# Soft mixture of experts: the first rows of x loaded in float32 on two hardware queues and cast on chip, with the opening matmuls in another order

## The chip, the cores and the metric

The kernel runs on one core of a Trainium2 chip. The metric is the device time of one execution in microseconds (us): the median of three runs. The profile is of one further execution, taken by the hardware profiler. Engines: TensorE (PE; PEld is its weight load), VectorE (DVE), ScalarE (ACT), GpSimd (POOL) and SyncE (SP). DMAs are issued by SyncE and ScalarE (hardware queues) and by GpSimd (a software queue, the only one used here for DMAs that change the type).

## What is computed

```python
# x: 16 x 512 x 512, router_logits: 16 x 512 x 8, expert_weights: 8 x 512 x 2048, all float32
probs = softmax(router_logits)             # over the 8 experts
for e in range(n_experts):
    expert_out = np.matmul(x, expert_weights[e])
    output += probs[:, :, e:e+1] * expert_out
```

Every row of x is scaled by each of its eight probabilities, and the eight scaled copies side by side (8 x 512 = 4096 columns) are multiplied by the stacked weights (4096 x 2048).

## The kernel before

All products are of float16 operands with float32 sums in PSUM. The 8192 rows are cut into 32 blocks of HQ = 256, and the whole multiplication is done by a fast scheme of seven block products at two levels (Strassen-Winograd). So x, weights, and sums and differences of weights are needed in many combinations; VectorE forms these while TensorE multiplies. That main part begins at about 42 us, has its order written out (from line 334 on), and is not changed in its text.

The change is in the opening, which is planned by hand:

- A zero tile is set on VectorE, and ten products of it (WARM, lines 84 to 89) run on TensorE into PSUM that is used by nothing else.
- Two small constants follow: ident (lines 209 to 212, set on VectorE, made an identity by GpSimd) and ones (line 257).
- The logits of the first four groups of 128 rows (lg0[0]) come in one DMA on SyncE (line 206). Rows 0 to 255 and 512 to 767 of x come in two DMAs of GpSimd (lines 207 and 208), which cast float32 to float16 on their way into the tile xs0. j numbers the groups: j = 0 and 1 are the first 256 rows, j = 2 and 3 the others.
- GpSimd then issues the first weights: the block b11[0, 0] for expert 0 in two halves (chunks c = 0, 1 and c = 2, 3 of 128 input columns), then whole experts. Two more casts of x (j = 4 to 7, lines 217 and 218) and further weights follow on the same queue.
- early_p(0) makes the softmax of these rows: VectorE with one exp on ScalarE.
- diag(p) writes, for one expert, four diagonal matrices of probabilities (ident times p), 128 x 512 in all.
- early_z0(e, d) makes, for expert e and each j, four small products (128 x 128) of x with such a diagonal. Their result in one bank of PSUM is x transposed and scaled. It is copied to z0[j] in float16, by VectorE for even j, by ScalarE for odd j (evacuate).
- Then comes the loop over n = 0, 1 (two column blocks of NB = 512) and e = 0 to 3 (HE = 4 experts). For each e, 16 large products (128 x 512), c outside and j inside, add z0[j] times the weights into four banks ps[j]. Before the change the small products of experts 0 and 1 stand ahead of the loop, those of experts 2 and 3 ahead of the large products of experts 0 and 1 of n = 0.
- At e = 2 of n = 0 the code writes down the two other softmaxes on VectorE: early_p(1), for j = 4 to 7, and softmax_of_all, for the logits of all rows. Their logits are loaded by load_logits on SyncE. softmax_of_all ends in two casts on ScalarE (lines 296 and 297) and four stores of the probabilities (p_dram) on SyncE.
- At the end of each n ScalarE copies the four banks out (line 331), and SyncE stores them (kept).
- In n = 1, behind the large products of experts 0 and 1, early_xp1 transposes x for j = 4 to 7 with ident, and spreads their probabilities with a product with ones (two banks for each j).

VectorE's and ScalarE's instructions of these helpers keep the order in which the code writes them (keep_in_program_order); TensorE executes in order too. PSUM has eight banks of 128 x 512 float32. bank() takes the next free one, and an instruction that needs a bank waits for whoever still reads it.

Of the kernel before, what the change touches and what calls it, by code (L numbers as in the profile page):

```python
# [31 lines left out]
def kernel(  # L32
# [7 lines left out]
    nc = tc.nc  # L40
    P = 128
    f16 = mybir.dt.float16
    f32 = mybir.dt.float32
# [3 lines left out]
    B, S, H = x.shape  # L47
    E, _, EH = expert_weights.shape
    T = B * S
    C = H // P  # L50
    HE = E // 2
    NB = 512
    NH = EH // 2
    WARM = 10
    HQ = 256
# [4 lines left out]
    x_f = x.flatten_outer_dims()  # L60
# [3 lines left out]
    wpool = ctx.enter_context(tc.tile_pool(name="wpool", bufs=15))  # L64
# [4 lines left out]
    cpool = ctx.enter_context(tc.tile_pool(name="cpool", bufs=1))  # L69
# [4 lines left out]
    def h_tile(shape, dtype):  # L74
        return hpool.tile(shape, dtype, name="h", tag="h")

    def half():
        return h_tile([P, NB], f32)

    tiny = cpool.tile([P, 1], f32, name="tiny")  # L80
    nc.vector.memset(tiny, 0.0)
    nc.scalar.activation(out=tiny, in_=tiny, func=mybir.ActivationFunctionType.Exp)

    with tc.tile_pool(name="psum0", bufs=1, space=bass.MemoryType.PSUM) as psum0:
        zero = h_tile([P, NB], f16)
        nc.vector.memset(zero, 0.0)
        every = psum0.tile([P, 8, NB], f32, name="every")
        for i in range(WARM):
            nc.tensor.matmul(every[:, i % 8, :], zero[:, 0:P], zero, start=True, stop=True)
# [5 lines left out]
    def note(i):  # L95
        last[i.ins.engine] = i.ins
        if ordered[0]:
            tc.keep_in_program_order(i)

    def dve(i):  # L100
        last[i.ins.engine] = i.ins
        tc.keep_in_program_order(i)

    act = dve
# [12 lines left out]
    def sp(o, i):  # L117
        note(nc.sync.dma_start(out=o, in_=i))

    def pool(o, i, **how):  # L120
        note(nc.gpsimd.dma_start(out=o, in_=i, **how))  # L121

    def bank():
        return psum.tile([P, NB], f32, name="ps", tag="ps")

    def mm(ps, z, w, start, stop):
        note(nc.tensor.matmul(ps, z, w, start=start, stop=stop, skip_group_check=True))  # L127
# [3 lines left out]
    def new_w():  # L131
        return wpool.tile([P, K8, NB], f16, name="w", tag="w")
# [31 lines left out]
    def inner_sums(b, t7=None):  # L164

        w = {1: b[0, 0], 2: b[1, 0], 3: b[1, 1], 7: t7 or b[0, 1]}

        def step(p, x, y):
            if p not in w:
                w[p] = new_w()  # L170
            tt(w[p], x, y, SUB)
        return w, {5: lambda: step(5, b[0, 1], b[0, 0]), 6: lambda: step(6, b[1, 1], w[5]),
                   4: lambda: step(4, b[1, 0], w[6]), 7: lambda: step(7, b[1, 1], b[0, 1])}
# [13 lines left out]
    lg_f = router_logits.flatten_outer_dims()  # L187
    P1, P2, PQ = 0, HE, 2 * HE

    xs0 = new_w()  # L190

    ROWS = ("(p j) h -> p j h", "(j p) h -> p j h")

    def cast_x(j):
        pool(xs0[:, ds(j, 2), :], x_f[ds(j * HQ, HQ), :].rearrange(ROWS[j // 4], p=P))

    def load_lg0(t):
        rows = lg_f.rearrange("(q h) e -> q h e", h=2 * HQ)[ds(2 * t, 2), 0:HQ]
        tile_ = lg0[t].rearrange("p (q j) e -> p q j e", j=2)
        if t == 0:  # L200
            sp(tile_, rows.rearrange("q (p j) e -> p q j e", p=P))
        else:
            for q in range(2):
                sp(tile_[:, q], rows[q].rearrange("(j p) e -> p j e", p=P))
    lg0 = [cpool.tile([P, 4, E], f32, name=f"lg0_{t}") for t in range(2)]
    load_lg0(0)
    cast_x(0)
    cast_x(2)
    ident = cpool.tile([P, P], f16, name="ident")
    nc.vector.memset(ident, 1.0)  # L210
    nc.gpsimd.affine_select(out=ident, in_=ident, compare_op=mybir.AluOpType.is_equal, fill=0.0, base=0,
                            pattern=[[-1, P]], channel_multiplier=1)
    b11 = {kn: new_w() for kn in BLOCKS}
    with behind():
        for kn in BLOCKS[:3]:
            cast_block(11, kn, b11[kn], 2 if kn == (0, 0) else 1)
    cast_x(4)
    cast_x(6)
    cast_block(11, BLOCKS[3], b11[BLOCKS[3]])

    def early_p(t):
        if t == 0:
            return softmax(lg0[t], 4, cpool.tile([P, HE, 4], f16, name="ph0"))
        pf = softmax(lg0[t], 4, cpool.tile([P, HE, 4], f32, name="pf0"))
        odd = pf.rearrange("p e (q j) -> p e q j", j=2)[:, :, :, 1]
        tt(odd[:, 0:2], odd[:, 0:2], odd[:, 2:4], ADD)
        ph = cpool.tile([P, HE, 4], f16, name="ph1")
        dve(nc.vector.tensor_copy(ph, pf))
        return ph

    def diag(p):

        d = h_tile([P, 4, P], f16)
        tt(d, ident.unsqueeze(1).to_broadcast([P, 4, P]), p.to_broadcast([P, 4, P]), MUL)
        return d

    def evacuate(o, ps, i):
        if i % 2:
            act(nc.scalar.copy(o, ps))
        else:  # L240
            dve(nc.vector.tensor_copy(o, ps))  # L241

    z0 = [zpool.tile([P, HE, C, P], f16, name="z", tag="z") for j in range(4)]
    ph0 = [early_p(0)]

    def diag_e(e):
        return diag(ph0[0][:, e].unsqueeze(2))

    def early_z0(e, d):
        for j in range(4):  # L250
            ps = bank()
            for c in range(C):
                mm(ps[:, ds(c * P, P)], xs0[:, j, ds(c * P, P)], d[:, j], c == 0, c == C - 1)
            evacuate(z0[j][:, e], ps.rearrange("p (c t) -> p c t", c=C), j)
# [5 lines left out]
    def diag_j(j):  # L260
        return diag(ph0[1][:, :, ds(j % 4, 1)])

    def early_xp1(j, d):
        t, rows = j // 2 - 2, ds(j % 2 * P, P)
        ps = bank()
        for c in range(C):
            mm(ps[:, ds(c * P, P)], xs0[:, j, ds(c * P, P)], ident, c == 0, c == C - 1)
        evacuate(xp1[t][0][:, :, rows], ps.rearrange("p (c t) -> p c t", c=C), 0)
        ps = bank()
        mm(ps, ones, d.rearrange("p e t -> p (e t)"), True, True)  # L270
        evacuate(xp1[t][1][:, :, rows], ps.rearrange("p (e t) -> p e t", e=HE), 1)
# [7 lines left out]
    def load_logits():  # L279
        dve(nc.vector.memset(lg_all[:, 0, 0:1], 0.0))  # L280
        dve(nc.vector.memset(lg0[1][:, 0, 0:1], 0.0))  # L281
        load_lg0(1)
        for r in range(R):
            sp(lg_all[ds(r * NHQ, NHQ)], lg_v[r])

    def softmax_of_all():

        pf = softmax(lg_all, J, h_tile([P, E, J], f32))
        pq = h_tile([P, HE, J], f32)
        tt(pq, pf[:, 0:HE], pf[:, HE:E], ADD)  # L290
        low = ds(P // 2, P // 2)
        pv = pf.rearrange("p (s e) j -> p s e j", s=2)[low]
        tt(pv[:, :, 0:2], pv[:, :, 0:2], pv[:, :, 2:4], ADD)
        tt(pq[low, 0:2], pq[low, 0:2], pq[low, 2:4], ADD)
        ph = h_tile([P, 3 * HE, J], f16)
        act(nc.scalar.copy(ph[:, 0:E], pf))
        act(nc.scalar.copy(ph[:, E:], pq))
        for r in range(R):
            sp(p_dram[:, :, ds(r * J, J)], ph[ds(r * NHQ, NHQ)])

    kept = [dram.tile([2, HQ, NB], f32, name=f"kept_{i}") for i in range(NI)]

    ds_ = [diag_e(0), diag_e(1)]
    early_z0(0, ds_[0])
    ds_.append(diag_e(2))
    load_logits()
    early_z0(1, ds_[1])
    for n in range(2):
        ps = [bank() for _ in range(4)]
        for e in range(HE):  # L310
            if n == 0 and e < 2:
                early_z0(e + 2, ds_[e + 2])
                if e == 0:
                    ds_.append(diag_e(3))
            if n == 0 and e == 2:
                ph0.append(early_p(1))
                ds_ = [diag_j(j) for j in range(4, 8)]
                softmax_of_all()
                w, sums = inner_sums(b11, new_w())
            for c in range(C):  # L320
                for j in range(4):
                    mm(ps[j], z0[j][:, e, c], b11[e // 2, n][:, e % 2 * C + c, :],
                       e + c == 0, e == HE - 1 and c == C - 1)
            if n == 1:
                for j in ((4, 5), (6, 7), (), ())[e]:
                    early_xp1(j, ds_[j - 4])
                if e == 1:
                    sums[5]()
        for j in range(4):
            o = half()  # L330
            act(nc.scalar.copy(o, ps[j]))
            sp(kept[j // 2][n].rearrange("(p j) m -> j p m", j=2)[j % 2], o)
# [706 lines left out]
```

## Time and profile before

| | |
|---|---|
| Median of three runs | 1377.12 us (1376.21 to 1377.82) |
| Profiled execution | 1377.86 us |
| Its span, from first to last instruction | 1376.2 us |
| TensorE busy | 1368.5 us (99%), 6390 matmuls |
| VectorE, ScalarE, GpSimd busy | 1108.8, 183.3, 412.3 us |
| Granted TensorE clock | 1.000 of full speed |

The opening in stretches: length, then TensorE's and VectorE's busy time and number of instructions, and the mean busy share of the 16 DMA engines (slightly over 1 where packets overlap).

| Stretch, us from the start | length | TensorE | VectorE | DMA share |
|---|---|---|---|---|
| 0.00 to 2.00 | 2.00 | 0.71 (2) | 0.61 (4) | 0.02 |
| 2.00 to 4.00 | 2.00 | 2.00 (6) | 0.86 (5) | 0.70 |
| 4.00 to 5.60 | 1.60 | 1.60 (5) | 1.35 (3) | 1.04 |
| 5.60 to 6.80 | 1.20 | 0.93 (9) | 0.40 (1) | 0.99 |
| 6.80 to 8.50 | 1.70 | 1.51 (24) | 1.45 (3) | 1.03 |
| 8.50 to 9.70 | 1.20 | 1.01 (16) | 1.20 (5) | 1.22 |
| 9.70 to 12.40 | 2.70 | 2.70 (15) | 1.95 (4) | 1.23 |
| 12.40 to 14.00 | 1.60 | 1.60 (19) | 0.35 (1) | 1.33 |

How to read it: matmuls are pipelined and the ends that the profile gives them are modelled, so a busy TensorE isn't TensorE at its peak. What counts is how far apart the starts of matmuls are. A line of the timeline has a start, a duration, the engine, the line of the code, the operation, and what it writes and reads; "x16" merges sixteen equal instructions, and the bracket tells how long the engine was idle before and what ended that. The chain of work goes back from the last instruction, at each step to what released it; a long chain through one engine means that this engine sets the end.

### The profile page before, as it was taken

How to read it: one execution, taken by the hardware profiler on the slowest of the kernel's cores; microseconds unless marked ns; L12 is line 12 of the kernel's file. 1: busy time of each engine (PE TensorE's matmuls, PEld its weight loads, DVE VectorE, ACT ScalarE, POOL GpSimd, SP SyncE). 2: the span in 40 equal slices, each digit the busy share in tenths (PEclk: the TensorE clock that was granted, in tenths of full speed). 3: DMA queues.
4: the chain of work that ended last, by engine and by line, in shares of the span. 5: the costliest groups of instructions: out<-in, count | busy, mean ns of one | idle time of the engine just before them, and what ended most of it. 6: DMA issues, size and time to landing. Idle time of an engine off the chain costs nothing.

```text
span 1376.2 us, 17481 instructions
## 1 busy us (share of the span) xinstructions
PE 1368.5 (99%) x6390; PEld 622.3 (45%) x6390; DVE 1108.8 (81%) x1290; ACT 183.3 (13%) x317; POOL 412.3 (30%) x652
## 2 busy tenths in 40 slices
PE   9999999999999999999999999999999999999998
PEld 4444444444444444444444444444444444444444
DVE  5846757679789888798887988889888898898782
ACT  3222111100011111111111100000000000222221
POOL 3222333231223342334332122333323322232321
PEclk9999999999999999999999999999999999999999
DMA  9997999999898998999897997988888979998785
GB/s 186 229 255 207 212 250 260 252 297 381 235 311 267 279 282 249 267 260 264 252 275 255 348 383 208 241 233 207 232 231 231 231 219 309 228 197 186 167 147 101
DMA packets 191271, 338.02 MB, mean 246 GB/s; under 512 B 52944, under 2 KB 86992, under 8 KB 187472
## 3 DMA queue, kind: packets, MB, share of 16 engines
q0 software_dynamic: 88688, 185.12, 55.8%
q1 hardware_dynamic: 98464, 123.34, 31.1%
q10 hardware_dynamic: 4032, 28.44, 5.3%
q8 instruction: 50, 0.82, 0.2%
q14 instruction: 37, 0.30, 0.1%
HBM read 207.65 MB, written 156.43 MB: 265 GB/s over the span
## 4 chain that ended last, share of the span: by engine, by line
PE 91%; issue 4%; DMA 3%; POOL 1%; DVE 1%; POOLq 0%; ACT 0%; DVEq 0%
PE ps L127 91%; POOL out_dram L121 1%; DMA out_dram<-h 1%; DMA w<-wd 1%; DMA w<-in_x_dram 0%; DVE h L107 0%; DVE z L107 0%; DVE u L107 0%; POOL wd L121 0%; DVE z L241 0%; POOL w L121 0%; ACT h L991 0%; POOLq L121 0%; DVEq L107 0%; DVE lg L281 0%
## 5 line engine op out<-in xcount | busy, mean ns | idle before, releaser
L127 PE MATMUL ps<-w,z 128*128 128x512 f16 x5416 | 1177.5, 379 | 2.1 <-DVE h L107 1.7
L127 PEld LDWEIGHTS <-z 128*128 128x128 f16 x5416 | 529.7, 98 | 639.8 <-issue 2.6
L121 POOL DMA_DIRECT2D out_dram<-h x380 | 249.2, 675 | 742.5 <-ACT h L536 369.1
L107 DVE TENSOR_TENSOR h<-ps,h 128x512 f32<-128x512 f32 x415 | 282.6, 688 | 207.8 <-PE ps L127 190.1
L107 DVE TENSOR_TENSOR z<-xT,pT 128x2048 f16<-128x2048 f16 x220 | 267.2, 1218 | 12.1 <-DMA xT<-xs 8.3
L127 PE MATMUL ps<-w,d 128*128 128x512 f16 x880 | 199.1, 379 | 0.0
L127 PEld LDWEIGHTS <-d 128*128 128x128 f16 x880 | 86.1, 98 | 103.8
L107 DVE TENSOR_TENSOR z<-z,d 128x2048 f16<-128x2048 f16 x110 | 132.2, 1217 | 0.0
L107 DVE TENSOR_TENSOR w<-w 128x1024 f16<-128x1024 f16 (+2 forms) x92 | 101.0, 1103 | 6.3 <-DMA wd<-w 3.9
L525 ACT COPY h<-ps 128x512 f32<-128x512 f32 x90 | 52.9, 587 | 375.0 <-PE ps L127 314.0
L536 ACT COPY h<-ps 128x512 f32<-128x512 f32 x64 | 37.6, 587 | 486.1 <-PE ps L127 459.7
L107 DVE TENSOR_TENSOR d<-z 128x1024 f16<-128x1024 f16 x110 | 75.4, 686 | 6.8 <-PE ps L127 5.0
L107 DVE TENSOR_TENSOR z<-z,u 128x2048 f16<-128x2048 f16 x64 | 78.4, 1225 | 2.2
L107 DVE TENSOR_TENSOR u<-xT,pT 128x2048 f16<-128x2048 f16 x64 | 78.0, 1219 | 0.0
L522 ACT COPY h<-ps 128x512 f32<-128x512 f32 x90 | 52.8, 587 | 173.8 <-PE ps L127 160.2
L121 POOL DMA_DIRECT2D wd<-w x86 | 48.4, 586 | 36.9 <-DVE w L107 27.4
L121 POOL DMA_DIRECT2D w<-in_expert_weights_dram x65 | 48.9, 783 | 34.2 <-DMA wd<-w 24.1
L107 DVE TENSOR_TENSOR ps<-ps,h 128x512 f32<-128x512 f32 (+1 forms) x66 | 45.4, 689 | 12.9 <-PE ps L127 12.9
L121 POOL DMA_DIRECT2D kept<-h x56 | 30.9, 551 | 75.5 <-ACT h L525 46.9
L107 DVE TENSOR_TENSOR h<-h 128x512 f32<-128x512 f32 (+2 forms) x69 | 45.1, 675 | 0.2
L518 ACT COPY ps<-ps 128x512 f32<-128x512 f32 x45 | 25.7, 572 | 114.6 <-PE ps L127 114.6
L107 DVE TENSOR_TENSOR z<-z 128x2048 f16<-128x2048 f16 x32 | 39.2, 1225 | 1.1
(47 smaller groups left out, 98.1 us busy)
## 6 DMA issues: line engine op xcount, KB each, us to landing
out_dram<-h POOLq DMA_DIRECT2D x380, 256.0 KB, 6.2
pT<-p_dram SPq DMA_DIRECT2D x140, 256.0 KB, 6.1
w<-wd ACTq DMA_DIRECT2D x27, 1024.0 KB, 9.8
h<-kept SPq DMA_DIRECT2D x100, 256.0 KB, 5.8
xT<-x SPq DMA_DIRECT2D x87, 256.0 KB, 5.8
wd<-w POOLq DMA_DIRECT2D x72, 256.0 KB, 5.8
w<-in_expert_weights_dram POOLq DMA_DIRECT2D x35, 512.0 KB, 10.1
h<-out_dram SPq DMA_DIRECT2D x68, 256.0 KB, 5.5
```

Source lines behind the costliest of these rows:

```text
L107: dve(nc.vector.tensor_tensor(out=o, in0=a, in1=b, op=op))
L121: note(nc.gpsimd.dma_start(out=o, in_=i, **how))
L127: note(nc.tensor.matmul(ps, z, w, start=start, stop=stop, skip_group_check=True))
L518: act(nc.scalar.copy(self.banks["b"], x))
L522: act(nc.scalar.copy(o[tn], q if p == 5 else x))
L525: act(nc.scalar.copy(o[TN[p]], b if p == 2 else x))
L536: act(nc.scalar.copy(o[tn], b))
```

## The change

- The two logits halves (128 x 16 each) and the two halves of x (256 rows each, 512 KB) for j = 0 to 3 are issued ahead of everything else, one of each on ScalarE's queue (j = 0, 1) and on SyncE's queue (j = 2, 3). x lands in float32 in the tile x32.
- GpSimd's two casting DMAs for these rows go; four copies cast x32 into xs0 instead, on ScalarE for j = 0 and 2, on VectorE for j = 1 and 3.
- The zero tile is kept (in the pool of the weights). In the built program its set stands on VectorE behind those of ident and ones.
- The small products of expert 0 are split in two groups: j = 0, 1, then three products of the zero tile; j = 2, 3, then one more.
- The 16 large products of expert 0 of n = 0 go by quarters (c = 0, 1 with j = 0, 1; c = 0, 1 with j = 2, 3; then the same with c = 2, 3). The small products of expert 1 stand after the first eight, those of expert 2 after the sixteen, those of expert 3 after the large ones of expert 1.

```diff
+    lg0 = [cpool.tile([P, 4, E], f32, name=f"lg0_{t}") for t in range(2)]
+    x32 = wpool.tile([P, 4, H], f32, name="x32", tag="w")
+    for q, begin in enumerate((nc.scalar, nc.sync)):
+        rows = ds(2 * q * HQ, HQ)
+        begin.dma_start(out=lg0[0][:, ds(2 * q, 2), :],
+                        in_=router_logits.flatten_outer_dims()[rows].rearrange("(p j) e -> p j e", p=P))
+        begin.dma_start(out=x32[:, ds(2 * q, 2), :], in_=x_f[rows, :].rearrange("(p j) h -> p j h", p=P))
     tiny = cpool.tile([P, 1], f32, name="tiny")
...
-        zero = h_tile([P, NB], f16)
+        zero = wpool.tile([P, NB], f16, name="zero", tag="w")
...
     def cast_x(j):
-        pool(xs0[:, ds(j, 2), :], x_f[ds(j * HQ, HQ), :].rearrange(ROWS[j // 4], p=P))
...
-    load_lg0(0)
-    cast_x(0)
-    cast_x(2)
+        pool(xs0[:, ds(j, 2), :], x_f[ds(j * HQ, HQ), :].rearrange("(j p) h -> p j h", p=P))
+
     ident = cpool.tile([P, P], f16, name="ident")
...
-    def early_z0(e, d):
-        for j in range(4):
+    def early_z0(e, d, js=range(4)):
+        for j in js:
...
-        load_lg0(1)
+        for q in range(2):
+            sp(lg0[1][:, ds(2 * q, 2), :], lg_f[ds((4 + 2 * q) * HQ, HQ)].rearrange("(j p) e -> p j e", p=P))
...
-    ds_ = [diag_e(0), diag_e(1)]
-    early_z0(0, ds_[0])
-    ds_.append(diag_e(2))
+    QUARTERS = [(c, j) for g in range(2) for h in range(2)
+                for c in (2 * g, 2 * g + 1) for j in (2 * h, 2 * h + 1)]
+    ORDERS = [(c, j) for c in range(C) for j in range(4)], QUARTERS
+
+    def cast_x32(j):
+        if j % 2:
+            dve(nc.vector.tensor_copy(xs0[:, j, :], x32[:, j, :]))
+        else:
+            act(nc.scalar.copy(xs0[:, j, :], x32[:, j, :]))
+
+    ds_ = [diag_e(0)]
+    for h in range(2):
+        for j in (2 * h, 2 * h + 1):
+            cast_x32(j)
+        early_z0(0, ds_[0], (2 * h, 2 * h + 1))
+        for i in range(3 - 2 * h):
+            mm(bank(), zero[:, 0:P], zero, True, True)
     load_logits()
-    early_z0(1, ds_[1])
+    ds_ += [diag_e(1), diag_e(2)]
     for n in range(2):
         ps = [bank() for _ in range(4)]
         for e in range(HE):
-            if n == 0 and e < 2:
-                early_z0(e + 2, ds_[e + 2])
-                if e == 0:
-                    ds_.append(diag_e(3))
+            if n == 0 and e == 1:
+                ds_.append(diag_e(3))
...
-            for c in range(C):
-                for j in range(4):
-                    mm(ps[j], z0[j][:, e, c], b11[e // 2, n][:, e % 2 * C + c, :],
-                       e + c == 0, e == HE - 1 and c == C - 1)
+            for c, j in ORDERS[n == 0 and e == 0]:
+                mm(ps[j], z0[j][:, e, c], b11[e // 2, n][:, e % 2 * C + c, :],
+                   e + c == 0, e == HE - 1 and c == C - 1)
+                ahead = {(0, 1, 3): 1, (0, 3, 3): 2, (1, 3, 3): 3}.get((e, c, j))
+                if n == 0 and ahead:
+                    early_z0(ahead, ds_[ahead])
```

## The prediction

> **What bounds the kernel now.** I read the page's chain of work first, then the chain in order of time, then the timeline of the first 29 us, then the landing times of DMAs.
>
> ```profile
> PE 91%; issue 4%; DMA 3%; POOL 1%; DVE 1%; POOLq 0%; ACT 0%; DVEq 0%
> ```
>
> TensorE sets the end. So time changes only where its stream of matmuls waits. In order of time:
>
> ```profile
> 2.00 4.86 DMA w<-in_x_dram
> ...
> 7.35 0.69 DVE z L241
> 8.04 0.60 DVE h L107
> ...
> 8.69 51.37 PE ps L127 x272
> ```
>
> Up to 8.7 us x and VectorE lead; after that TensorE alone. The timeline (start, duration) of the opening:
>
> ```profile
> 0.97 0.27 DVE L86 MEMSET h<- 128x256 uint32 x1
> 1.21 0.17 DVE L210 MEMSET ident<- 128x128 f16 x1
> 1.29 4.45 PE L89 MATMUL every<-h 128*128 128x512 f16 x10 [1.29 <-DVE h L86]
> ...
> 2.90 5.24 POOL L121 DMA_DIRECT2D w<-in_expert_weights_dram  x7
> ...
> 5.64 0.77 PEld L127 LDWEIGHTS <-w 128*128 128x128 f16 x8 [0.80 <-DMA w<-in_x_dram]
> ...
> 6.91 1.51 PE L127 MATMUL ps<-h,w 128*128 128x128 f16 x24 [0.33 <-DMA w<-in_x_dram]
> ...
> 7.57 1.56 ACT L239 CAST z<-ps 128x512 f16<-128x512 f32 x3 [0.36 <-PE ps L127]
> ...
> 9.75 2.27 PEld L127 LDWEIGHTS <-z 128*128 128x128 f16 x12 [0.17 <-DMA w<-in_expert_weights_dram]
> ```
>
> Spacing, from count and duration less the last one's (0.22 small, 0.38 large, 0.63 warming, single rows): a warming product 0.424, a small one (1.51-0.22)/23 = 0.056, a large one 0.216 (51 in 11.17). 48 small products end the opening; the first large one starts at 9.76, held 0.15 by its weights, and no wait follows in this stretch. Then the part that no chain shows, because it is just in time:
>
> ```profile
> 13.64 1.29 DVE L241 CAST z<-ps 128x512 f16<-128x512 f32 x2 [2.00 <-PE ps L127]
> ...
> 15.19 0.19 DVE L177 TENSOR_REDUCE h<-lg 128x4 f32<-128x32 f32 x1 [0.26 <-DMA lg<-in_router_logits_dram]
> ...
> 24.82 0.62 ACT L296 CAST h<-h 128x512 f16<-128x512 f32 x1 [3.37 <-DVE h L107]
> ...
> 25.65 2.04 ACT L331 COPY h<-ps 128x512 f32<-128x512 f32 x4
> ...
> 27.93 0.39 PE L127 MATMUL ps<-ident,w 128*128 128x128 f16 x4
> ```
>
> VectorE runs both remaining softmaxes without a break from 15.19; ScalarE's casts (L296) wait for their end; behind these, in order, stand the four copies (L331) that empty the banks of n = 0; early_xp1 takes these banks at 27.93. The first copy ends at 25.65+0.58 = 26.23: 1.7 us of slack.
>
> **The change, part by part. The start.** The zero tile is now set behind the two other constants on VectorE. Their spacing is 0.14 (L210 at 1.21, the next at 1.35), so it is 0.28 late: warming starts at 1.58, and its ten products hold TensorE until 1.58+10x0.427 = 5.85 (without the last one's tail).
>
> **x.** Two issues, the logits' first, stand on ScalarE and SyncE. Logits took 0.46 and the next SyncE issue stood at 1.33, so both halves of x are issued near 1.33. On ScalarE some 0.9 us of issuing goes ahead of the table load (1.28): exp moves from 3.18 to about 3.35, hidden, since its diagonal is ready near 5.0 and TensorE is busy to 5.85. Neither two such loads nor a 4 KB piece of float32 stand in the trace. Bounds:
>
> ```profile
> lg<-in_router_logits_dram SPq DMA_DIRECT2D x1, 16.0 KB, 1.9
> ...
> kept<-h SPq DMA_DIRECT2D x4, 256.0 KB, 2.5
> ...
> DMA to landing us min/median/max: 4.9/9.8/17.0
> ```
>
> The first two are single stretches of the DMA view; the last is the 1 MB fetch on ScalarE's queue. From below: one half alone, 1.9+0.6x2 = 3.1, lands at 4.5. Both together are 1 MB: 1.9+0.6x4 = 4.3, so 5.6; by the fetch's best, 4.9, so 6.2. I take 5.95, between the last two, as the engines carry both halves at once and the weights soon after (their share is 1.04 in 4.0 to 5.6 us already). From above 9.8, the fetch's median.
>
> The Trainium skill (DMA: Bandwidth & Descriptors, "Issuing engines are not separate DMA queues") says that transfers begun by ScalarE, SyncE and GpSimd share the same 16 DMA engines and interleave, so that two queues save issue time alone. By it the 1 MB figure holds for both halves; were the queues independent, the sum below would fall to its floor. No run yet shows two hardware queues here.
>
> **Cast and small products.** A cast f16<-f32 of this size on ScalarE is L296, 0.62; hand-overs are 0.04 to 0.05 (product ends 6.36, VectorE starts 6.40). On VectorE it is unpriced: between 0.18 (L228, 128x16) and 0.69 (out of PSUM), hidden under ScalarE's either way. With x at t: cast done t+0.66, eight products from t+0.71, the second group ends t+1.32; its copy to z starts t+1.36; ScalarE's next operation follows 0.48 later (three in 1.56): cast of j = 2 from t+1.84 to t+2.46; products of j = 2, 3 from t+2.51 to t+2.96. Three of the new products (0.65) fill a wait of 1.35 and cost nothing; the fourth costs 0.22. First large product: t+3.17 = 9.12 (at 5.85 for the products' start, the floor, 8.31).
>
> The clock: small spacing falls from 0.107 to 0.056 near 6.2 us, 4.9 after warming began. TensorE's waits here stay under 1.4; idle of 0.49 (before 6.91) left it at 0.056. So the four products gain nothing. The Trainium skill (TensorE: Matmul & The Clock Gate, "What's actually happening") puts the release at about 3.4 us of activity in windows that run free of the kernel; by it, as an estimate, the release could fall at 5.0 us, which x's landing hides, or some 3.4 us later than in the trace, at the price of a half-speed start.
>
> **Weights.** GpSimd loses two casts (1.26 of issuing): weights start near 1.6, not 2.90, land 6.8 after at the soonest, 8.4, and are hidden by 0.7. Later weights keep their slack (the second half landed at 11.0, needed then at 11.5; now needed 9.12+2.6).
>
> **Moved work.** 32 small products, of experts 1 and 2, come after the first large ones: 32x0.056 = 1.79. So 9.12 now stands against 9.76-1.79 = 7.97 before: **+1.15**.
>
> **The cover that goes.** Expert 3's small products move behind all large ones of expert 1. They start at 9.12 + 32x0.216 + 32x0.056 = 17.8, not 13.22, and VectorE's two copies of them stand ahead of the softmaxes: as before they begin 0.43 and 1.03 after, the softmax 1.63 after, at 19.45 (15.19 before). The next logits, issued near 9.4 for 8.7 and 5.8 in flight, are there. The chain up to the first emptied bank, 26.23-15.19 = 11.04, is all VectorE and ScalarE: 30.5 with the hand-over. TensorE comes there at 17.8+0.9+48x0.216 = 29.1. A wait of 1.46 takes the slack's place; the next two banks (0.48 apart) add some 0.12: **+1.58**. It does not depend on when x lands, both sides move together. What waits behind: stores of p, 4.3 late; their readers stood at 42.05, 6.5 after the last landed (35.6), and move 2.7 too.
>
> At nothing: SyncE's extra issue; tiles exchanged between pools (free since 6 us); x of j = 4 to 7, landed 25.8 and 27.1, needed 27.9 and 32.0.
>
> **Sum.** +1.15+1.58 = +2.73. The profiled execution took 1377.86 for a span of 1376.2, thus 1380.6 for one like it; it lies 0.74 above the median. On the median of 1377.12: **1379.85**.
>
> **Rivals.**
> - Not slower: the late softmaxes do not reach TensorE, by a bank free earlier or ScalarE ready sooner; only +1.15 is left: **1378.3**. It decides if the wait is under 1.58. For: the slack was 1.7. Against: ScalarE and VectorE keep their written order, and all eight banks are in use.
> - Faster: x at 4.5 and the clock up by 4.3 us: first large product at 7.7, -0.3, and no bank wait: **1376.8**. Against: two things at once.
> - Collision: x on loaded engines takes the fetch's median, 9.8: t = 11.1, +5.2 more: **1385**. Decides from 0.2% on wherever t exceeds 5.97. For: weights start 1.3 earlier and share 1.04. Against: up to 4 us the share is 0.70.
> - The change does not do what it says: the first weights land as before, 9.7, and set the start: 9.76, +0.64: **1380.5**.
>
> **How the numbers follow.** 0.2% is 2.75 us, about what a measurement can tell from no change; the forecast lies at that edge. Chances: forecast 0.56, split evenly by the edge; not slower 0.14; faster 0.07; collision 0.10; weights 0.13, two thirds beyond the edge. Faster by over 0.2% needs -2.75, which no case gives: 0.02 for what I miss. Slower: 0.28+0.10+0.09 = 0.47; within: 0.51. Range: from 1377.8 (below the floor of 8.31, which gives +1.9, towards 1378.3 and half a us of scatter) to 1382.0 (t = 8).
>
> **What would show it.** Right: first small product near 6.7; the first large near 9.1; ScalarE's copies of n = 0 near 30; a TensorE wait of some 1.5 before the ident products, released by ScalarE. Wrong: large products before 8.0, or those ident products without a wait.

## The result and the profile after

The changed kernel is slower. Its median is 1382.36 us (9 runs, 1380.45 to 1386.72) beside 1377.07 for the kernel before in the same comparison (9 runs, 1376.21 to 1379.12). The ratio is 1.0034 with a 95% interval of 1.0025 to 1.0043, which is 4.7 us; the two medians themselves lie 5.29 apart. The forecast was 1379.85, that is +2.73; its direction is right and its size is short by 2 to 2.6. The median lies 0.36 above the upper end of the stated range, 1382.0; the ratio put on the median the forecast started from, 1377.12, gives 1381.8, just inside. The forecast itself is below every execution of the changed kernel on record (14, the fastest 1380.45).

The profiled execution took 1382.62 for a span of 1380.82, and the one before 1377.86 for 1376.16: 4.66 more. The chain that ended last still belongs to TensorE. The page of the changed kernel gives it by engine:

```profile
PE 91%; issue 4%; DMA 2%; POOL 1%; DVE 1%; ACT 0%; ACTq 0%; POOLq 0%; DVEq 0%
```

The same chain in order of time (start, duration, what) shows what leads the opening:

```profile
1.25 5.33 DMA x<-in_x_dram
...
6.60 0.63 ACT w L305
```

Before, x and VectorE led up to 8.7. Now the float32 x leads to 6.58, and ScalarE's cast (L305) stands behind it on the chain. The new loading does not bring x sooner where it counts: the halves landed at 5.60 and 6.87 before and land at 6.39 and 6.58 now, and the first small product moves from 5.80 to 7.27. The timeline of the changed kernel (start, duration, engine, line, operation; the bracket is the idle time ahead and what ended it):

```profile
1.47 5.35 POOL L128 DMA_DIRECT2D w<-in_expert_weights_dram  x7
...
1.57 4.45 PE L96 MATMUL every<-zero 128*128 128x512 f16 x10 [1.57 <-DVE zero L93]
...
6.60 0.62 ACT L305 CAST w<-x 128x512 f16<-128x512 f32 x1 [3.16 <-DMA x<-in_x_dram]
6.60 0.47 DVE L303 CAST w<-x 128x512 f16<-128x512 f32 x1 [1.72 <-DMA x<-in_x_dram]
...
7.27 0.62 PE L134 MATMUL ps<-h,w 128*128 128x128 f16 x8 [1.25 <-ACT w L305]
...
9.09 0.86 PE L134 MATMUL ps<-h,w 128*128 128x128 f16 x8 [0.55 <-ACT w L305]
...
10.17 3.16 PE L134 MATMUL ps<-w,z 128*128 128x512 f16 x8
...
20.56 1.29 DVE L234 CAST z<-ps 128x512 f16<-128x512 f32 x2 [2.46 <-PE ps L134]
...
21.77 0.17 DVE L184 TENSOR_REDUCE h<-lg 128x4 f32<-128x32 f32 x1
...
32.20 2.04 ACT L339 COPY h<-ps 128x512 f32<-128x512 f32 x4
...
32.92 0.38 PE L134 MATMUL ps<-ident,w 128*128 128x128 f16 x4 [1.37 <-ACT h L339]
```

Three things are to be read here. First, TensorE waits 1.25 for the first cast and 0.55 for the third, and its first large product starts at 10.17. Second, the eight large products from 10.17 on take 3.16, where eight at the spacing of the kernel before (0.216) would take 1.9. Third, the softmax of the next logits starts at 21.77 (15.19 before), ScalarE's copies of the banks at 32.20 (25.65), and the ident products wait 1.37 for them; before they stood at 27.93 with no wait.

The second point is the clock. The view by windows, of the changed kernel, has for each stretch its length, the busy time (and instructions) of PE, PEld, DVE, ACT and POOL, the granted clock, the DMA share and GB/s:

```profile
5.91:9.32 3.41, 1.61 (x16) 0.89 (x16) 1.50 (x3) 1.72 (x3) 2.26 (x4) 1.00 1.18 182
9.32:12.73 3.41, 3.41 (x15) 1.45 (x12) 1.91 (x5) 0.59 (x1) 1.07 (x3) 0.50 1.24 207
```

In the 3.41 us ahead of 9.32 TensorE was busy for 1.61; in the next 3.41 us the granted clock is 0.50. That stretch does half the work: 3.41 x 1/2 = 1.7 us lost.

The first ident product is a good mark for the sum, because everything up to it is the opening. It moved from 27.93 to 32.92, by 4.99: the start as forecast 1.15; x later than forecast 6.58-5.95 = 0.63; the clock 1.71; the wait before the bank 1.53 (1.746 between the starts less 0.216). That makes 5.02. Behind this mark TensorE's waits for over 0.1 us are the same in both traces but for one of 0.56 at 799.6 (0.4 by the modelled ends), for weights that ScalarE fetches back, which the changed kernel doesn't have; the stretch behind the last matmul is 0.21 longer. 4.99-0.56+0.21 = 4.64, of 4.66.

### The profile page after: what moved, and what is told of

It reads as the page before. It is cut to its first block, busy times and chain, and to the rows that moved or that the text cites. A ratio compares the mean times of both kernels' runs of the same rounds, so it can differ in the third digit from the quotient of the medians.

```text
span 1380.8 us, 17496 instructions
## 1 busy us (share of the span) xinstructions
PE 1370.6 (99%) x6394; PEld 622.9 (45%) x6394; DVE 1109.4 (80%) x1292; ACT 184.2 (13%) x319; POOL 410.8 (30%) x650
## 4 chain that ended last, share of the span: by engine, by line
PE 91%; issue 4%; DMA 2%; POOL 1%; DVE 1%; ACT 0%; ACTq 0%; POOLq 0%; DVEq 0%
PE ps L134 91%; DMA out_dram<-h 1%; POOL out_dram L128 1%; DVE h L114 1%; DMA x<-in_x_dram 0%; POOL wd L128 0%; DVE z L114 0%; DVE u L114 0%; DVE z L234 0%; ACT w L305 0%; DVE h L188 0%; DVE h L189 0%; DVE h L184 0%; ACT h L186 0%; ACT z L232 0%
```

## The experiments

The theory after the result was: the new order of expert 3 causes the wait before the bank, and the two waits for casts together drop the clock. The rivals: the products of the zero tile cost something; the loading, not the order, makes the loss; and x lands late because the weights now share the DMA engines with it. This table has all twelve runs made after the result, with values from each one's profiled execution; "x landed" is the landing of the later half. Large products of the kernels that keep the order of before stand behind 32 more small ones, so their first large product is to be compared with 9.76, that of the others with 9.76-1.79 = 7.97. Each ratio is to the kernel before on the same chip; its median was 1377.91 beside the first four kernels of the table after the changed one, 1378.02 beside the next four and 1377.49 beside the last four.

| kernel | x landed | first large product | wait before the first bank | first ident product | span | median | ratio to before, 95% |
|---|---|---|---|---|---|---|---|
| before | 6.87 | 9.76 | none | 27.93 | 1376.16 | 1377.07 | 1 |
| changed | 6.58 | 10.17 | 1.53 | 32.92 | 1380.82 | 1382.36 | 1.0034 (1.0025 to 1.0043) |
| e3_sooner | 6.98 | 10.97 | none | 30.92 | 1380.27 | 1379.92 | 1.0016 (1.0008 to 1.0025) |
| warm14 | 6.44 | 9.62 | 1.53 | 31.09 | 1378.57 | 1380.71 | 1.0018 (1.0009 to 1.0027) |
| no_zero_between | 6.26 | 9.50 | 1.53 | 32.39 | 1379.84 | 1382.51 | 1.0031 (1.0019 to 1.0042) |
| x_by_gpsimd | 7.08 | 10.01 | 1.53 | 31.49 | 1378.90 | 1380.72 | 1.0024 (1.0014 to 1.0034) |
| load_only | 6.66 | 11.77 | none | 29.93 | 1378.75 | 1379.21 | 1.0005 (0.9996 to 1.0013) |
| load_only_w_later | 6.71 | 11.73 | none | 29.89 | 1378.49 | 1378.88 | 1.0006 (0.9998 to 1.0015) |
| change_w_later | 6.54 | 9.73 | 1.44 | 31.12 | 1379.11 | 1380.88 | 1.0022 (1.0013 to 1.0030) |
| warm14_e3_sooner | 6.58 | 9.90 | none | 29.85 | 1378.89 | 1379.58 | 1.0011 (1.0002 to 1.0020) |
| change_again | 6.56 | 9.74 | 1.53 | 31.22 | 1378.91 | 1381.85 | 1.0032 (1.0019 to 1.0045) |
| one_queue | 6.00 | 12.01 | 1.53 | 34.34 | 1381.35 | 1383.61 | 1.0047 (1.0034 to 1.0059) |
| half_each | 5.93 | 10.61 | none | 28.77 | 1376.41 | 1379.01 | 1.0010 (1.0001 to 1.0019) |
| half_each_diags | 6.07 | 11.79 | none | 30.40 | 1379.09 | 1380.18 | 1.0016 (1.0008 to 1.0025) |

### Does the late softmax make the wait? (e3_sooner)

Expert 3's small products go back in front of expert 1's large ones; all else is the changed kernel.

```diff
-                ahead = {(0, 1, 3): 1, (0, 3, 3): 2, (1, 3, 3): 3}.get((e, c, j))
+                ahead = {(0, 1, 3): 1, (0, 3, 3): 2, (1, 1, 3): 3}.get((e, c, j))
```

> The changed kernel with expert 3's small products behind the first eight large ones of expert 1, not behind all sixteen. Theory (the wait of 1.4 us before the first ident product, at 31.2 in the changed kernel, comes from the softmaxes that stand on VectorE behind expert 3's copies): the softmaxes start 8 x 0.216 = 1.73 us sooner, at about 20.0 instead of 21.8, the wait ends under 0.1, and the span falls by 1.4 to 1.5, to some 1379.3 if the clock behaves as in the changed kernel's profile (1377.6 if it does not fall). Rival (the banks are late only because the opening as a whole is late, by x and the clock): the wait stays above 1 us and the span at 1380.8. A second rival (the wait is hidden elsewhere anyway): the wait goes, but another of the same length appears before 60 us.

The timeline of e3_sooner around the first ident products:

```profile
30.00 2.04 ACT L339 COPY h<-ps 128x512 f32<-128x512 f32 x4
...
30.92 0.39 PE L134 MATMUL ps<-ident,w 128*128 128x128 f16 x4
31.14 0.38 PE L134 MATMUL ps<-h,ones 128*128 128x512 f16 x1
31.60 0.38 PE L134 MATMUL ps<-ident,w 128*128 128x128 f16 x4
32.09 0.38 PE L134 MATMUL ps<-h,ones 128*128 128x512 f16 x1
```

The first ident product has no bracket: it doesn't wait. The softmax starts at 19.57 (21.77 in the changed kernel) and the copies of the banks at 30.00, 0.92 ahead of the product. The later banks are now just in time: starts are 0.46 and 0.49 apart where 0.22 is the spacing, so 0.24 and 0.27 remain of the wait. The ratio falls from 1.0034 to 1.0016. The execution that was profiled ran at half speed up to 10.95, which is why its span says little; the medians carry the verdict on the time (the two intervals only touch). So the wait follows from the place of expert 3's small products: shown. The small waits before later banks were a miss of the expectation.

### Is it the clock? (warm14, no_zero_between, change_again)

Four more warming products, which end nearer to x's landing:

```diff
-    WARM = 10
+    WARM = 14
```

> The changed kernel with 14 opening products instead of 10. Theory (TensorE's idle 1.45 us before x's casts, together with 0.9 before the second group, lets the granted clock fall to 0.5 for one window of 3.4 us, 9.3 to 12.7): the products run to about 6.9, small ones still start near 7.3, no stretch at 0.50 follows, the large products start 0.427 apart nowhere, and the span falls by 1.5 to 1.9, to about 1379.0; the median falls by as much if most executions have the fall. Rival (the fall belongs to the moment or to the load, not to the idle time): a stretch at 0.50 stays, span 1380.8. Second rival (more opening products delay the small ones): small ones start after 7.5, span 1381 or more.

In the view by windows of warm14 the clock is up over the same stretch as above, and the eight large products from 9.62 on take 1.89:

```profile
7.27:9.30 2.03, 1.48 (x18) 0.87 (x17) 1.02 (x2) 1.10 (x2) 0.65 (x2) 1.00 1.20 196
9.30:12.70 3.40, 3.40 (x33) 2.10 (x31) 2.84 (x7) 1.29 (x3) 1.06 (x2) 1.00 1.24 206
```

In 9.30 to 12.70 there are 33 matmuls, against 15 in the changed kernel's. The median falls to 1.0018, and the bank wait is still 1.53, as it has to be if it does not depend on when the opening starts.

The products of the zero tile between the small ones are taken out:

```diff
-        for i in range(3 - 2 * h):
-            mm(bank(), zero[:, 0:P], zero, True, True)
```

> The changed kernel without the four zero products between the small ones. Theory (they fill only part of a wait and don't keep the clock up): the clock falls in the same window as with them, the first large product is 0.43 sooner (the fourth product at half speed), span 1380.4. Rival (they hold the clock for some of the time): without them the half-speed stretch begins sooner or lasts two windows, span 1382 or more. If no fall shows in this execution, neither is told apart by the span, and the spread of the times has to tell.

```profile
5.51:8.92 3.41, 1.09 (x13) 0.60 (x12) 1.80 (x3) 1.72 (x3) 2.07 (x4) 1.00 1.12 177
8.92:12.33 3.41, 3.41 (x15) 1.64 (x14) 1.91 (x5) 0.59 (x1) 1.41 (x2) 0.50 1.24 205
```

These are windows of no_zero_between: with TensorE busy for 1.09 in one window, the next is at half speed. With the products (1.61 busy) the changed kernel lost the same window. The ratio is 1.0031, with an interval that covers the changed kernel's. The four products gain nothing that can be measured. A cost doesn't show either, but one under 1 us would be lost in these intervals: the fourth product stands ahead of the first large one and takes 0.43 of the changed kernel's trace (9.74 to 10.17, at half speed; 0.22 at full).

The changed kernel once more, with no edit, is to show how much the clock alone changes between executions:

> The changed kernel once more, beside the following runs. Theory (the granted clock falls to 0.5 for a window of 3.4 us in those executions whose window catches about 2 us of TensorE's idle time): the ratio lies near 1.003 again, the wait for the banks is 1.5 in this profile too; where the clock does not fall, the first large product is at 9.7 and the span near 1378.8 to 1379.2, where it falls 10.2 or later and 1380.8. Rival (the half-speed stretch of the first profile was a chance of that execution): no fall here, and the ratio 1.002 or less.

```profile
6.63:10.04 3.41, 2.24 (x22) 1.40 (x23) 2.00 (x4) 1.99 (x4) 1.96 (x4) 1.00 1.17 182
10.04:13.45 3.41, 3.41 (x30) 2.00 (x29) 2.66 (x7) 1.34 (x3) 1.14 (x2) 1.00 1.24 207
```

In this execution the clock rose at 6.63 instead of 5.91. The edge of a window now cuts the first wait for a cast (6.02 to 7.25) in two, the window after 6.63 is filled to 2.24, and the clock stays up. The span is 1378.91, 1.91 less than the first profile of the same kernel, of which the clock explains 1.71. The first ident product moved by 31.22-27.93 = 3.29 = 1.15 (start) + 0.61 (x) + 1.53 (bank wait). So one kernel loses 1.7 us or not by where the windows of the clock fall, and its median (1381.85 here) lies between.

### The order or the loading? (x_by_gpsimd, load_only, warm14_e3_sooner)

x_by_gpsimd has the new order and the new zero products, but loads x and the logits as before, without the four casts; its logits and x go by these lines:

```diff
+    sp(lg0[0].rearrange("p (q j) e -> p q j e", j=2),
+       lg_f.rearrange("(q h) e -> q h e", h=2 * HQ)[ds(0, 2), 0:HQ].rearrange("q (p j) e -> p q j e", p=P))
+    cast_x(0)
+    cast_x(2)
...
-        for j in (2 * h, 2 * h + 1):
-            cast_x32(j)
```

> The changed order of products, with the four zero products, but x and the logits loaded as before the change (two casting DMAs on GpSimd, one logits DMA on SyncE, no copies that cast). Theory (order and loading cost separately): x lands near 5.6 and 6.9 as before, the second group of small products is through by 8, the first large one waits for its weights to about 9.7, as before; 32 small products are still to come (+1.8), and the wait for the banks stays (+1.4): span 1376.2 + 3.2 = 1379.4, and 1381 if the idle 1.5 us before the weights lets the clock fall. Rival (the loading alone makes the loss): span 1376.5 or less, no wait before the ident products.

Its timeline of TensorE:

```profile
5.44 0.62 PE L127 MATMUL ps<-h,w 128*128 128x128 f16 x8 [0.23 <-DMA w<-in_x_dram]
...
10.01 1.89 PE L127 MATMUL ps<-w,z 128*128 128x512 f16 x8 [2.05 <-DMA w<-in_expert_weights_dram]
```

The small products start 1.8 earlier than in the changed kernel, and that is worth nothing: TensorE then waits 2.05 for the first weights, which land at 9.88. Before, the 32 small products of experts 1 and 2 hid that landing. The new order takes them away, so it needs earlier weights, which only the new loading gives. The order alone costs 1.0024 (3.3 us).

load_only is the other half: the order of before, the new loading, four casts in front of the first small products.

```diff
     ds_ = [diag_e(0), diag_e(1)]
+    for j in range(4):
+        if j % 2:
+            dve(nc.vector.tensor_copy(xs0[:, j, :], x32[:, j, :]))
+        else:
+            act(nc.scalar.copy(xs0[:, j, :], x32[:, j, :]))
     early_z0(0, ds_[0])
```

> The order of products of the kernel before, with the changed loading alone: x in float32 on two hardware queues, four casts one behind the other (two on each engine) ahead of the small products, no zero products, weights 1.4 us sooner on GpSimd. Theory (the change's order is most of the loss, the loading alone costs little): x lands at 6.3 to 6.8, the 48 small products start near 7.2 and run without a wait over 0.5, the first large one starts at 10.0 to 10.4 (9.76 before), no wait before the ident products; span 1376.5 to 1376.9, and up to 1.7 more if the clock falls or rises late. Rival (the loading is the loss): first large product after 11, span 1379 or more at full clock.

```profile
7.35 4.58 PE L134 MATMUL ps<-h,w 128*128 128x128 f16 x48 [1.33 <-ACT w L302]
11.77 2.54 PE L134 MATMUL ps<-w,z 128*128 128x512 f16 x11
```

In the execution of load_only that was profiled the clock rose only at 11.00, so the 48 small products took 4.4 and the first large one came at 11.77, not near 10 as expected. The median is 1.0005, an interval that holds no change. There is no wait before the bank. So the loading by itself is about neutral, and the order by itself costs 3.3 us: the order carries most of the loss. That 1.0005 and 1.0024 come near the 1.0034 of both is in part chance, because the starts are late for different reasons: x_by_gpsimd's by 10.01-7.97 = 2.04 for the weights, the changed kernel's for x and its casts. The wait of 1.53 before the bank is the same in both.

Both repairs in one kernel, 14 warming products and expert 3's small products sooner, are the edits of warm14 and e3_sooner together:

> The changed kernel with both of the runs before: 14 opening products, and expert 3's small ones behind the first eight large ones of expert 1. If the two losses are separate, they add: no half-speed stretch, first large product near 9.6, no wait over 0.2 before the ident products, span 1377.2 to 1377.8, thus 1 to 1.6 over the kernel before and 1.4 below warm14 (1378.6). Rival (the bank wait is only moved): span 1378.6 as in warm14.

It has 1.0011. The clock rose at 6.87 and stayed; the first ident product at 29.85 waits for nothing, the next banks 0.25 and 0.27. The median is 1.56 over the kernel before, within the expected 1 to 1.6; the expected span was missed (1378.89 for 1377.2 to 1377.8). By the ratios the two repairs do not add: 0.0018 and 0.0016 apart, 0.0023 together. The start is 9.90-7.97 = 1.93 late. Of this 0.63 is x and 1.15 is what was forecast; the rest is the longer warming itself, whose fourteen products at half speed hold TensorE to 7.43, where the first small product stood at 7.25 to 7.27 with ten.

### Why does x land at 6.58? (load_only_w_later, change_w_later, one_queue, half_each, half_each_diags)

The prediction took 5.95 and named sharing with the weights as the reason for a later landing. Two kernels hold the weights back behind a fill on GpSimd, one with the order of before and one with the new order; the edit is the same:

```diff
-    with behind():
+    hold = nc.gpsimd.memset(xs0[:, ds(4, 4), :], 0.0)
+    with tc.issue_after(hold.ins):
         for kn in BLOCKS[:3]:
```

> As load_only, with a fill of half of xs0 on GpSimd (128x2048, overwritten by its later casts) ahead of the weights, so that these are issued one to two us later. Theory (x on the hardware queues lands at 6.4 only because the weights share the 16 DMA engines with it): x lands by 5.7, small products start by 6.5, the first large one at 9.2 or at the weights' landing, if that is later; span 1375.5 to 1376.2. Rival (1 MB on two queues takes 5 us from its issue, whoever else is there): x still at 6.2 or later, weights later too, span 1377 or more.

> The changed kernel with the same fill on GpSimd ahead of its weights. Theory of sharing: x by 5.7, first small product by 6.5, TensorE idle under 0.7 us before it, so the clock does not fall, first large product near 9.0, the wait for the banks stays at 1.5; span 1378.3 to 1378.8. Rival (inherent): x at 6.2 or later, span 1380 or more.

GpSimd's timeline of change_w_later shows the weights' issues 1.70 later than in the changed kernel:

```profile
1.42 1.79 POOL L207 MEMSET w<- 128x2048 f16 x1
3.17 5.35 POOL L128 DMA_DIRECT2D w<-in_expert_weights_dram  x7
```

The landing of x's two halves, counted from their issue, is the same line in its view of in_x_dram as in the changed kernel's:

```profile
DMA to landing us min/median/max: 5.1/5.2/5.3
```

The weights were still held only to 3.17, and x was on its way to 6.5, so the DMA view of the changed kernel itself has to settle it. From 1.2 to 5.9 it has these queues, SyncE's (q1) and ScalarE's (q10), each with packets, MB and share:

```profile
q1 hardware_dynamic: 316, 0.53, 43.5%
q10 hardware_dynamic: 276, 0.52, 35.0%
```

GpSimd's queue (q0) is missing: the weights, issued at 1.47, had no packet on the DMA engines before 5.96, when nearly all of x was through (its last packet is at 6.06). So sharing with the weights is not the reason; this theory falls. Of the 5.33 us from issue to landing, 1.1 pass before x's first packet (2.34), 3.7 up to its last one, and 0.5 from there to the landing. The ratio of change_w_later is 1.0022; its clock stayed up (2.19 busy in the window), and it keeps the wait before the bank (1.44, then 0.05 and 0.06). load_only_w_later tells the same of x (6.71 and 6.53), and gives another case of the clock: busy 1.24 of the window up to 7.72, then half speed up to 11.13. Its median is 1.0006.

Then the queues. one_queue sends both halves of x on SyncE's queue and both of the logits on ScalarE's:

```diff
-    for q, begin in enumerate((nc.scalar, nc.sync)):
+    for q in range(2):
...
-        begin.dma_start(out=lg0[0][:, ds(2 * q, 2), :],
+        nc.scalar.dma_start(out=lg0[0][:, ds(2 * q, 2), :],
...
-        begin.dma_start(out=x32[:, ds(2 * q, 2), :], in_=x_f[rows, :].rearrange("(p j) h -> p j h", p=P))
+        nc.sync.dma_start(out=x32[:, ds(2 * q, 2), :], in_=x_f[rows, :].rearrange("(p j) h -> p j h", p=P))
```

> The changed kernel with both halves of x on SyncE's queue, one behind the other, and both logits halves on ScalarE's. Theory (two queues bring no bandwidth, both halves of the change land late together): the first half lands by 5.2, the second at 6.3 to 6.6 as in the change; small products start at the end of the warming ones, 5.9, TensorE idles 0.3 or less before them, the clock stays up, the first large product near 9.0, the wait for the banks stays; span 1378.0 to 1378.5. Rival (one queue is slower than two): the first half after 6, the second after 7.5, span 1381 or more.

From issue to landing of the logits' two halves in one_queue:

```profile
DMA to landing us min/median/max: 4.0/4.5/4.9
```

x does come sooner: its halves land at 4.61 and 6.00, because nothing is issued ahead of them. But the 8 KB halves of the logits need 4.0 and 4.9, though they stand on a queue of their own; issued ahead of x, the half on ScalarE's queue needed 1.9. The softmax starts at 6.29 and the diagonal at 7.71, TensorE idles 2.80, the clock comes up only at 13.72, and the kernel is the slowest of all, 1.0047. The expected gain at x was there and lost to the logits. From the first issue to the last landing both ways take about as long, 6.00-0.81 = 5.2 on one queue and 6.58-1.25 = 5.3 on two.

half_each splits the work by kind: rows of j = 2, 3 in float32 on SyncE's queue, with two casts; rows of j = 0, 1 by GpSimd's casting DMA as before; the order of before.

```diff
+    nc.sync.dma_start(out=x32, in_=x_f[ds(2 * HQ, HQ), :].rearrange("(p j) h -> p j h", p=P))
...
-    load_lg0(0)
+    nc.scalar.dma_start(out=lg0[0].rearrange("p (q j) e -> p q j e", j=2),
+                        in_=lg_f.rearrange("(q h) e -> q h e", h=2 * HQ)[ds(0, 2), 0:HQ].rearrange("q (p j) e -> p q j e", p=P))
     cast_x(0)
-    cast_x(2)
...
+    act(nc.scalar.copy(xs0[:, 2, :], x32[:, 0, :]))
+    dve(nc.vector.tensor_copy(xs0[:, 3, :], x32[:, 1, :]))
```

> The kernel before with one half of x changed: rows 512 to 767 come in float32 on SyncE's queue, issued first, with two casts on chip; the other half and all weights stay on GpSimd, where one casting DMA less stands ahead of the weights; the first logits come on ScalarE's queue. Order of products as before, no zero products between. Theory (what the change meant to gain is there if no half waits for the other): both halves by 5.8, second group of small products at 6.3 to 6.6 (6.91 before), the first weights by 9.0 (9.71 before); the first large product is then set by the diagonal of expert 2, near 9.2; span 1375.5 to 1375.8. Rival (512 KB on a hardware queue take 4 us or more beside GpSimd's): second half after 6, first large product at 9.7 or later, span 1376 to 1377.

> As half_each, with the diagonals of experts 0, 1 and 2 all made before x is there, so that the small products of expert 2 need not wait for one (0.49 before). Theory: the 48 small products run from 5.8 to 8.8, the first large one starts with the landing of its weights, 8.7 to 9.2; span 1375.2 to 1375.6, below the kernel before. Rival (the third diagonal, 0.60, delays the cast on VectorE and the copies of z behind it): first large product after 9.5, no gain over half_each.

x is there at 4.56 and 5.93, the earliest of all these kernels. But the logits land 4.0 after their issue again, and VectorE's timeline of half_each shows what that leads to:

```profile
4.79 0.19 DVE L180 TENSOR_REDUCE h<-lg 128x4 f32<-128x32 f32 x1 [3.27 <-DMA lg<-in_router_logits_dram]
...
6.22 1.29 DVE L110 TENSOR_TENSOR h<-ident,ph 128x512 f16<-128x512 f16 x2
```

The diagonals start at 6.22, so the first small product stands at 7.06 in spite of the early x. The median is 1.0010. Nor do the two kinds of loading run side by side here: GpSimd's half of x, issued at 1.34, has its first packet at 3.93, when SyncE's half has its last (3.97). half_each_diags only puts the third diagonal ahead of the casts; it lost a window to the clock (9.28 to 12.69, after a window with 1.53 busy) and has 1.0016. Its ratio tells nothing of the diagonal by itself, but its timeline shows the rival of the expectation, a cast on VectorE held up by the diagonal (it starts at 8.02, 7.43 in half_each):

```profile
8.58 3.42 PE L130 MATMUL ps<-h,w 128*128 128x128 f16 x36 [0.71 <-DVE w L307]
```

No kernel of these beats the one before: load_only and load_only_w_later come nearest and can't be told from it. A kernel like half_each with the logits issued ahead of x was not run.

## Why the prediction was right and wrong

- The start of the warming, 1.58: it is 1.57. Right.
- x at 5.95: it landed at 6.58. This term of the start was mis-sized by 0.63. It was set between 5.6 (a line through two small transfers) and 6.2 (the best of the 1 MB fetches, 4.9); two halves on two hardware queues took 5.1 and 5.3 here. Sharing with the weights, one of its reasons for going as high as 5.95, is not the cause: they moved nothing before 5.96. The rule weighed there, that two queues save issue time alone, agrees with the runs: 5.2 on one hardware queue, 5.3 on two (GpSimd's queue, which it counts in, did not interleave with them; see the last section). Why 1 MB takes that long in this place stays open.
- The path from x to the first large product: t+0.71 for the first small one is t+0.69; t+2.51 for the second group is 9.09 = t+2.51. VectorE's cast, unpriced between 0.18 and 0.69, is 0.47 and 0.42, under ScalarE's 0.62 as said. With x where it was, 9.12 becomes 9.75, and change_again has 9.74.
- "TensorE's waits here stay under 1.4 ... So the four products gain nothing". The second half came out right, as no_zero_between shows, but not for the reason given: the clock did fall, and the products were too few to hold it. The step that failed is the first: it judged each wait by itself (by its own terms 0.8 before the first group, from 5.85 to t+0.71, and 1.35 less 0.65 before the second) against an idle time of 0.49 that had left the clock up. The waits (1.25 and 0.55) fell in one window of 3.41 us, the clock dropped for the next one, and 1.7 us were lost. This is the missing term of the sum. It belongs to some executions and not to all: change_again lost none.
- The weights: forecast 8.4, landed at 8.38, and hidden. That rival, the weights as before, falls; x_by_gpsimd shows what it would have looked like (9.88, wait of 2.05).
- The cover that goes: +1.46 for the first bank and 0.12 for the next two, forecast together as 1.58. Measured 1.53, nearly all at the first bank (0.01 and 0.06 follow), in six executions whose first ident product stands anywhere from 31.09 to 34.34. Expert 3's small products, the softmax and the copies all came later than forecast (20.14 for 17.8, 21.77 for 19.45), both sides by about 2.3 (0.63 of x and 1.7 of the clock), so the wait stayed: "It does not depend on when x lands" held, and e3_sooner shows the cause.
- "At nothing": not quite. A wait of 0.56 near 800 us, for weights fetched back, is in the trace of before and not in that of the changed kernel, and stands with 0.83 in e3_sooner's and 0.81 in load_only's. What decides it stays open; the prediction had not looked that far down.
- The rivals. "Not slower" needed a bank wait well under 1.58, "faster" x at 4.5: both fall. The collision put x at 9.8; it landed at 6.58. But the point from which that case was said to pass 0.2%, t over 5.97, was passed, and the time went with it.

The profile of change_again, with the clock up, is 2.75 longer in span than before; the forecast's sum was 2.73. That is not all to its credit: x cost 0.61 more, while the wait near 800 us gave 0.56 back and one near 1180 us, 0.50 in the trace of before, is 0.25 shorter. The near agreement is in part luck.

## What to carry to other kernels

Work that stands ahead of its need is often the cover for something else: the small products moved here hid the weights' landing and kept the softmaxes ahead of the bank copies, so moving them cost more than it could bring, the more so as the new loading let the small products start no sooner (7.27, before 5.80). Before an opening is reordered, follow what each moved result releases on the other engines down to the next point that is just in time, and add up all of TensorE's idle time in any 3.4 us rather than judging each wait alone. A difference of 1 to 2 us in one execution of such a kernel can be the clock's phase alone, so compare medians, and look at the clock before a trace is read.

## What the runs showed of the hardware

- The granted clock moves in steps of one window of 3.41 us whose phase differs between executions: it rose between 4.31 (load_only_w_later) and 13.72 (one_queue). The Trainium skill (TensorE: Matmul & The Clock Gate, "What's actually happening") describes such a free-running window, and says that the rate falls back after at least one idle window. Here it fell after windows that were partly busy: 1.61, 1.09, 1.24 and 1.53 of 3.41 (changed, no_zero_between, load_only_w_later, half_each_diags). It stayed up after 2.24 (change_again), 2.19 (change_w_later) and 2.06 (half_each). Ahead of the first rise the view by windows prints 1.00 as well; there the spacing of the warming products, 0.43 where large ones at full clock stand 0.216 apart, tells that the clock is at half. Counted back from the first rise in steps of 3.41, the window ahead of it has TensorE busy for 2.73 or more in all fourteen profiles; the windows that no rise followed have 2.60 or less.
- A busy share alone doesn't decide it. x_by_gpsimd, with large products instead of small ones in the busy part, kept the clock after 1.37:

```profile
7.94:11.36 3.42, 1.37 (x8) 0.67 (x8) 1.53 (x5) 0.43 (x1) 1.61 (x3) 1.00 1.21 197
11.36:14.77 3.41, 3.41 (x35) 2.23 (x34) 1.29 (x2) 1.07 (x2) 1.30 (x2) 1.00 1.29 227
```

  What is counted in a window stays open. That small products count for less than large ones would fit, and so would that it matters where in the window the busy part lies; neither was tested.
- A small transfer beside a large one waits, though it has a queue of its own. The logits on ScalarE's queue, issued at 0.81 as x was on SyncE's, took 4.0 (half_each, and the first half in one_queue); issued on both queues ahead of x they took 1.8 and 1.9 in the changed kernel. The Trainium skill (DMA: Bandwidth & Descriptors, "Queues, rings and completion order") says that each DMA engine takes turns between queues after every packet. The packets agree. In one_queue x comes in 256 packets of 4 KB and the logits in 256 of 64 bytes, and from 3 to 5 us SyncE's queue (q1) and ScalarE's (q10) sent nearly the same number:

```profile
q1 hardware_dynamic: 206, 0.78, 95.7%
q10 hardware_dynamic: 196, 0.01, 6.6%
```

  With turns by packet, 8 KB of small rows last as long as 512 KB of large ones: the halves of the logits land at 4.79 and 6.19, those of x at 4.61 and 6.00.
- GpSimd's queue did not come into these turns. Its first packet comes as the float32 loads on the hardware queues run out: at 5.96 (changed; their last at 6.06), 5.10 (one_queue; 5.40) and 3.93 (half_each; 3.97), though issued at 1.47, 1.36 and 1.34. Before the change, without such loads, it came at 2.74 after an issue at 1.33. Why stays open.
